# A retention scores step moved, the GroupNorm root in a step of its own, and other first loads and last root, in a two-layer recurrent decoder step

## The chip, the cores and the metric

The kernel runs on one core of one Trainium2 chip, in one launch. The time is device microseconds of an execution, as a median over runs; the profile is one execution recorded on the chip, and its times are microseconds from the start of its span.

## What is computed

One inference step of a hybrid decoder trunk for 256 prompt tokens and 8 x 8 sample tokens, 320 in all, in float32. Each of two layers normalises `x` (2048 wide), projects it with one wide matrix, runs three recurrent branches beside each other, projects each back, weighs the three with sigmoid gates and adds the result to `x`. A last RMSNorm follows. Cut to what the change touches:

```python
def _retention(q, k, v, r0, pos0, gn_g):          # 8 heads, 128 wide, chunks of 128 (or 8) positions
    q = _rope(q, pos); k = _rope(k, pos) * (RET_DK ** -0.5)
    def step(r, inp):
        qc, kc, vc = inp
        sc = jnp.einsum('bihd,bjhd->bhij', qc, kc) * dmask[None]             # scores
        inner = jnp.einsum('bhij,bjhe->bihe', sc, vc)
        cross = jnp.einsum('bihd,bhde->bihe', qc, r) * xi[None, :, :, None]
        r_new = r * g_chunk + jnp.einsum('bjhd,bjhe->bhde', kc * zeta, vc)   # state
        return r_new, inner + cross
    r_last, o = lax.scan(step, r0, (chunks of q, k, v))
    o = ((o - mu) * lax.rsqrt(var + GN_EPS)) * gn_g                          # GroupNorm per head
    return o, r_last

def _layer(x, ...):
    xn = _rmsnorm(x, norm_g)
    proj = xn @ w_in                     # 2048 x 14336: inputs, gate paths and merge gates of all branches
    y_s5, y_lru, y_ret = _s5(...), _rglru(...), _retention(...)
    b_m = (y_m * silu(z_m)) @ w_branch_m          # for the three branches
    merged = sum over m of sigmoid(g_m) * b_m
    return x + merged @ w_out

y = _rmsnorm(x, final_norm_g)            # behind the second layer; the new states are returned too
```

## The kernel before

Tokens lie along the free axis (320), features along the 128 partitions. All large weights stream through the core once. They come in chunks of 512 KB, four k-tiles of 128 by 256 outputs (`raw`, four buffers, issued on SP at L1234). Since the products are to be exact in float32, each half of a chunk is split into a rounded part `whi` (ACT, L126) and a remainder `wlo` (DVE, L99); `prep` and `split` do that into four buffers. Each k-tile and each half of the outputs then takes three matmuls of 128x320: `whi` by the high part of the activations, `whi` by their low part, `wlo` by their high part (L1321, L1322, L1323). A chunk is 24 matmuls.

The order of all engines' work is written by the loop in `stream`, chunk by chunk; the program's scheduler leaves it as it is. `blocks` lists the weight blocks of a layer: inputs of the LRU and S5 branches, gates, then for m = 0 to 3 a pair of retention heads with its q, k, v and z block of four chunks each (16 chunks for each m), the S5 gate path, merges, the GLU, merges, and the output projection. Splits run three halves ahead of the matmuls for most of the program, loads three chunks ahead. After each chunk `self.step()` advances every generator in `self.gens` by one `yield`; so all side work is dealt out in steps of one chunk, and what stands between two yields of a generator is issued in one lump. A block's handler starts one step after its last chunk.

Generators that the change touches or that stand beside it: `ret_qk` rotates q or k: it copies the block out of PSUM (`rraw`), starts the product `ra`, swaps halves of partitions by two DMAs (`rsw`, L840 and L841), multiplies and adds (`ra`, DVE). `ret_heads` loads the decay masks (`rdms`, `rdm`), makes a padded copy `kd` of the keys, then the scores (L894, L895, L898, each set in PSUM of its own), masks them on DVE (`scs`, `rsc`), transposes the keys, loads the old states `r0`, makes the heads' output, its GroupNorm statistics (`bs`, `mv`, L960 and L961), the GroupNorm root (`gv`, a chain of small DVE operations) and the normalised output (`ron`). Behind the statistics it spawns `ret_state`, which makes the new states: L1004, the store `ret_p` (L1018), then four times a pair of masked values `rvm` (DVE), a pair of matmuls L1029 into PSUM and the update `r` (DVE, L119), and after each head the store `ret_s` (L1033, on SP, so it stands in line with the loads of `raw`). The loads of `r0` for the next m wait until `ret_state` of this one has ended. Small PSUM tiles come from a pool of four, main accumulators from a pool of two.

At the start, `constants` and `more_constants` load the vectors `pv` and small tables on ACT's queue, `x` and the first chunk come in alternation on SP, and `x_group(0)` splits the first activations before `prep(0)` splits the first weights. At the end `finish` takes the sum of squares (L1100 adds the last ones), makes the reciprocal root (`ts` on DVE, Ln and Exp on ACT, three DVE operations), multiplies the eight output tiles `yt` (fourteen DVE operations, two on POOL, L1117) and stores each (`y`, L1120).

## Time and profile before

| | before |
|---|---|
| median of 3 runs | 2405.69 us (2404.81 to 2407.02) |
| profiled execution | 2406.62 us, span 2404.8 us |
| mean granted TensorE clock | 0.995 |
| busy | PE 2360.1, DVE 1572.1, ACT 1070.8, POOL 605.9 us |
| HBM | 373.83 MB read, 31.74 MB written, 169 GB/s over the span |

In the profile PE is the matmul engine, DVE the vector engine, ACT the scalar engine, POOL GpSimd, and SP the engine on whose queue most DMAs are issued (SPq). An entry `wlo<-raw,whi` names what an operation writes and reads. PEclk is the share of full clock that TensorE was granted: 1.00 is 2.4 GHz, 0.50 is 1.2 GHz. "Idle before" is the time an engine stood before an operation, with the operation that released it. The tables of waits count such times by line.

### The profile page before, as it was taken

The numbers are of one execution on the slowest core, as the hardware profiler recorded it, in microseconds if no ns is written. First come the engines' busy times: TensorE is split into PE (matmuls) and PEld (weight loads), VectorE is DVE, ScalarE is ACT, GpSimd is POOL, SyncE is SP. The second block draws the span as 40 slices with busy tenths as digits, with TensorE's granted clock in tenths as the row PEclk, the third lists the DMA queues.
The fourth block names the chain that finished last, engine by engine and source line by source line (L and its number), as shares of the span: only waits on it lengthen the run. The fifth ranks groups of instructions, "written<-read, shape, count | busy, mean of one in ns | idle before, by whom it ended". The sixth has DMA issues, their size and how long they took to land.

```text
span 2404.8 us, 44311 instructions
## 1 busy us (share of the span) xinstructions
PE 2360.1 (98%) x16746; PEld 2326.9 (97%) x16746; DVE 1572.1 (65%) x2900; ACT 1070.8 (45%) x1941; POOL 605.9 (25%) x1157
## 2 busy tenths in 40 slices
PE   8999999999999999999999999999999999999997
PEld 8999999889999999999999999999999999999997
DVE  7889466876774756755567665767776656555544
ACT  6655344333343434444555554433333334444443
POOL 2004001999920000300100000699950200000011
PEclk9999999999999999999999999999999999999998
DMA  6655587454654545446656587454555554444553
GB/s 213 220 173 166 159 218 211 126 172 159 193 171 164 168 151 173 152 151 195 201 165 190 162 223 206 147 182 137 168 170 168 178 184 157 149 153 146 158 179 118
DMA packets 153590, 413.71 MB, mean 172 GB/s; under 512 B 18592, under 2 KB 59296, under 8 KB 153120
## 3 DMA queue, kind: packets, MB, share of 16 engines
q1 hardware_dynamic: 152656, 410.58, 54.1%
q8 instruction: 131, 2.15, 0.4%
q14 instruction: 83, 0.68, 0.1%
q10 hardware_dynamic: 720, 0.30, 0.0%
HBM read 373.83 MB, written 31.74 MB: 169 GB/s over the span
## 4 chain that ended last, share of the span: by engine, by line
PE 95%; DVE 3%; DMA 1%; issue 0%; ACT 0%; SPq 0%; ACTq 0%; DVEq 0%
PE pt L1321 30%; PE pt L1323 29%; PE pt L1322 29%; DMA raw<-w_in 1%; PE ps L638 1%; PE ps L757 1%; DVE wlo L99 1%; DVE rvm L99 1%; PE ps L546 1%; PE ps L1029 1%; PE ps L894 0%; PE ps L953 0%; ACT whi L126 0%; DVE yt L99 0%; PE ps L1004 0%
## 5 line engine op out<-in xcount | busy, mean ns | idle before, releaser
L99 DVE TENSOR_TENSOR wlo<-raw,whi 128x512 fp32r<-128x512 f32 x1187 | 845.5, 727 | 758.1 <-ACT whi L126 737.4
L126 ACT ACTIVATE whi<-raw 128x512 fp32r<-128x512 f32 x1187 | 737.7, 629 | 1071.3 <-PE pt L1322 894.2
L1321 PE MATMUL pt<-xh,whi 128*128 128x320 f32 x3320 | 1037.5, 313 | 6.1 <-ACT whi L126 6.1
L1323 PE MATMUL pt<-xh,wlo 128*128 128x320 f32 x3320 | 1029.8, 310 | 7.6 <-DVE wlo L99 7.5
L1322 PE MATMUL pt<-xl,whi 128*128 128x320 f32 x3320 | 1027.6, 310 | 0.0
L1321 PEld LDWEIGHTS pt<-xh,whi 128*128 128x128 f32 x3320 | 625.6, 188 | 11.8 <-ACT whi L126 6.4
L1323 PEld LDWEIGHTS pt<-xh,wlo 128*128 128x128 f32 x3320 | 625.0, 188 | 11.5 <-DVE wlo L99 11.3
L1322 PEld LDWEIGHTS pt<-xl,whi 128*128 128x128 f32 x3320 | 625.4, 188 | 2.8
L1321 PE MATMUL pt<-yhl,whi 128*128 128x320 f32 x756 | 234.7, 310 | 0.0
L1323 PE MATMUL pt<-yhl,wlo 128*128 128x320 f32 x756 | 233.6, 309 | 0.0
L1322 PE MATMUL pt<-yhl,whi 128*128 128x320 f32 x756 | 233.6, 309 | 0.0
L563 POOL TENSOR_TENSOR cs<-H,l2r 128x64 f32<-128x64 f32 x254 | 121.2, 477 | 255.6 <-DVE H L113 235.9
L252 POOL TENSOR_TENSOR acc<-acc,sq 128x320 f32<-128x320 f32 x28 | 25.6, 914 | 586.4 <-ACT sq L126 585.4
L1321 PE MATMUL pt<-M,whi 128*128 128x320 f32 x512 | 158.7, 310 | 0.0
L1323 PE MATMUL pt<-M,wlo 128*128 128x320 f32 x512 | 158.2, 309 | 0.0
L1322 PE MATMUL pt<-M,whi 128*128 128x320 f32 x512 | 158.2, 309 | 0.0
L1321 PEld LDWEIGHTS pt<-yhl,whi 128*128 128x128 f32 x756 | 141.9, 188 | 0.8 <-issue 0.5
L1322 PEld LDWEIGHTS pt<-yhl,whi 128*128 128x128 f32 x756 | 141.9, 188 | 0.0
L1323 PEld LDWEIGHTS pt<-yhl,wlo 128*128 128x128 f32 x756 | 141.9, 188 | 0.0
L565 POOL TENSOR_TENSOR cs<-cs,H 128x64 f32<-128x64 f32 x254 | 132.3, 521 | 0.0
L564 POOL TENSOR_TENSOR cs<-H,l2i 128x64 f32<-128x64 f32 x254 | 123.8, 487 | 0.0
L566 POOL TENSOR_TENSOR H<-cs,cs 128x64 f32<-128x64 f32 x254 | 117.7, 463 | 19.9
(251 smaller groups left out, 2526.5 us busy)
## 6 DMA issues: line engine op xcount, KB each, us to landing
raw<-w_in SPq DMA_DIRECT2D x447, 512.0 KB, 4.4
raw<-w_out SPq DMA_DIRECT2D x64, 512.0 KB, 4.5
raw<-wb_lru SPq DMA_DIRECT2D x32, 512.0 KB, 4.7
raw<-wb_ret SPq DMA_DIRECT2D x32, 512.0 KB, 3.8
raw<-wb_s SPq DMA_DIRECT2D x32, 512.0 KB, 3.6
r<-sret SPq DMA_DIRECT2D x16, 512.0 KB, 8.0
ret_s<-r SPq DMA_DIRECT2D x16, 512.0 KB, 3.0
raw<-w_glu SPq DMA_DIRECT2D x16, 512.0 KB, 3.6
```

The source lines that it names most:

```text
L99: self.nc.vector.tensor_tensor(o, a, b, op=op)
L126: self.nc.scalar.activation(o, a, f, **k)
L252: self.nc.gpsimd.tensor_tensor(self.acc, self.acc, sq, op=OP.add)
L546: self.nc.tensor.matmul(pp[g][:, a * HN:(a + 1) * HN], wst[:, a, g * 128:(g + 1) * 128], ust[:, 2 * a + g], start=True, stop=True, skip_gr ...
L563: g.tensor_tensor(t1, old, lr, op=OP.mult)
L564: g.tensor_tensor(t2, self.swap(old), li, op=OP.mult)
L565: g.tensor_tensor(t1, t1, new, op=OP.add)
L566: g.tensor_tensor(new, t1, t2, op=OP.add)
L638: nc.tensor.matmul(o[q * 32:(q + 1) * 32], w[:, c, m], H[:, q0 + m, c, col:col + HN], start=col == 1 and c == 0, stop=c == 1, tile_positio ...
L1321: nc.tensor.matmul(o, hi[:, kk, cs], xh, start=k == 0, stop=False)
L1322: nc.tensor.matmul(o, hi[:, kk, cs], xl, start=False, stop=False)
L1323: nc.tensor.matmul(o, lo[:, kk, cs], xh, start=False, stop=k == nk - 1)
```

## The change

In words: (1) `ret_heads` has one more `yield` between the padded copy of the keys and the scores; the third score product goes to the last 128 columns of the first score tile, so that two PSUM tiles are taken and not three. (2) A `yield` between the GroupNorm statistics and the root; `ret_state` is spawned behind the root and its yield. (3) At the start: eight products of `ones` with itself on PE (L216); the first `x` group and `pv` on ACT's queue, in the pieces column 0, `pv`, column 1, columns 2 and 3; the first chunk in four parts on SP; the first weights are split by k-tile between the pieces of `x`, and the first half chunk's matmuls go by k-tile; the tables `ident`, `sm`, `pmask` and the second `pv` are loaded on SP after chunk 8. (4) At the end: `rsqrt_of` takes the root with one activation function on ACT (its table is loaded earlier) and three DVE operations, the last of which leaves the root in PSUM; DVE multiplies from there, ACT copies it to SBUF for POOL, which has four of the sixteen multiplications now.

```diff
@@ -207,23 +207,24 @@
         pc = self.pc
         for l in range(DEPTH):
             self.pv[l] = pc.tile([128, NPV], F32, name=f"pv{l}")
-        nc.scalar.dma_start(self.pv[0], I['pv'][0])
         self.ones = pc.tile([128, 128], F32, name="ones")
         nc.vector.memset(self.ones, 1.0)
         self.fv = self.pl.tile([128, 4, 4], F32, name="fv", tag="fv")
         nc.vector.memset(self.fv, 1.0)
+        p = self.ps()
+        for _ in range(8):
+            nc.tensor.matmul(p[:, :128], self.ones, self.ones, start=True, stop=True)
 
     def more_constants(self):
         nc, I = self.nc, self.I
-        self.table_of(AF.Ln)
         self.ident = self.pc.tile([128, 128], F32, name="ident")
         self.sm = self.pc.tile([128, NK], F32, name="sm")
         self.pmask = self.pc.tile([128, 128], F32, name="pmask")
-        nc.scalar.dma_start(self.ident, I['c_ident'])
-        nc.scalar.dma_start(self.sm, I['c_sm'])
-        nc.scalar.dma_start(self.pmask, I['c_pair'])
+        nc.sync.dma_start(self.ident, I['c_ident'])
+        nc.sync.dma_start(self.sm, I['c_sm'])
+        nc.sync.dma_start(self.pmask, I['c_pair'])
         for l in range(1, DEPTH):
-            nc.scalar.dma_start(self.pv[l], I['pv'][l])
+            nc.sync.dma_start(self.pv[l], I['pv'][l])
 
     def pcol(self, l, key, i):
         c = PV[key] + i
@@ -275,10 +276,16 @@
         self.stt(r, t, 1.5, r, OP.add, OP.mult)
 
     def rsqrt_of(self, p):
+
         r = self.pl.tile([128, T], F32, name="rstd", tag="rstd")
-        for _ in self.rsqrt_steps(p, r):
-            pass
-        return r
+        v, t, q = (self.vt([128, T]) for _ in range(3))
+        rp = self.ps()[:, :T]
+        self.act(q, p[:, :T], AF.Abs_reciprocal_sqrt, scale=1.0 / D, bias=self.fv[:, 2, 0:1])
+        self.ts(v, p[:, :T], 1.0 / D, OP.mult, EPS, OP.add)
+        self.mul(t, q, q)
+        self.stt(t, t, -0.5, v, OP.mult, OP.mult)
+        self.stt(rp, t, 1.5, q, OP.add, OP.mult)
+        return r, rp
 
     def rs2(self, n=2):
         return self.rstd[:, None, :].to_broadcast([128, n, T])
@@ -286,11 +293,17 @@
     def x_load(self, q):
         a = self.py.tile([128, 4, T], F32, name="xin", tag="y")
         self.xin[q] = a
+        if q == 0:
+            for c in range(2):
+                self.nc.scalar.dma_start(a[:, c], self.I['x'][0][:, c])
+                yield
+            self.nc.scalar.dma_start(a[:, 2:4], self.I['x'][1])
+            return
         for h in range(2):
             self.nc.sync.dma_start(a[:, 2 * h:2 * h + 2], self.I['x'][2 * q + h])
             yield
 
-    def x_group(self, q):
+    def x_group(self, q, step=2):
 
         for c in range(4):
             k = 4 * q + c
@@ -300,7 +313,7 @@
             self.copy(xh, x, scale=g)
             self.stt(xl, x, g, xh.bitcast(F32), OP.mult, OP.subtract)
             self.xh[k], self.xl[k] = xh, xl
-            if c % 2:
+            if c % step == step - 1:
                 yield
 
     def x_rest(self, q):
@@ -888,14 +901,15 @@
         q, k = self.ret.pop(('q', m)), self.ret.pop(('k', m))
         kd = self.vt([128, 2, 2, 64], name="rkd")
         self.copy(kd, k[:, :, None, SEQ:].to_broadcast([128, 2, 2, 64]))
+        yield
         pp, sc = [], []
         for n in range(2):
             p = self.ps()
             nc.tensor.matmul(p[:, :256], k[:, n, 0:128], q[:, n, 0:256], start=True, stop=True)
             nc.tensor.matmul(p[:, 256:384], k[:, n, 128:256], q[:, n, 128:256], start=True, stop=True)
             pp.append(p)
-        p = self.ps()
-        nc.tensor.matmul(p[:, :128], kd.rearrange("p n r t -> p (n r t)")[:, 64:192], q[:, :, SEQ:], start=True, stop=True)
+        p = pp[0][:, 384:]
+        nc.tensor.matmul(p, kd.rearrange("p n r t -> p (n r t)")[:, 64:192], q[:, :, SEQ:], start=True, stop=True)
         yield
         scs = self.scs
         for n in range(2):
@@ -960,7 +974,7 @@
                 nc.vector.bn_stats(bs[:, s], o[:, s])
                 nc.vector.bn_aggr(mv[:, n, s], bs[:, s])
         self.flag['av', l, m] = True
-        self.spawn(self.ret_state(l, m, kt, kz, vt, vs, r0))
+        yield
         vv = self.pl.tile([128, 3, 6], F32, name="gv", tag="gv")
         v, rs, t = (vv[:, i] for i in range(3))
         gp = sm[:, K_GP + 6 * m:K_GP + 6 * m + 6]
@@ -970,6 +984,7 @@
         self.rsqrt_vec(rs, v, t)
         self.mul(rs, rs, gp)
         yield
+        self.spawn(self.ret_state(l, m, kt, kz, vt, vs, r0))
         on = []
         for n in range(2):
             x = self.wt([128, 3, 128], name="ron")
@@ -1083,7 +1098,8 @@
                 self.sumsq(y[:, n])
                 self.copy(y[:, n], y[:, n], scale=self.pcol(l, 'fin', 2 * j + n))
             if j == 5:
-                self.table_of(AF.Ln)
+                self.nc.vector.memset(self.fv[:, 2, 0:1], EPS)
+                self.table_of(AF.Abs_reciprocal_sqrt)
             if j == 6:
                 yield 3
                 p = self.fsum = self.ps()
@@ -1107,16 +1123,18 @@
 
     def finish(self):
         nc, O = self.nc, self.O
-        r = self.rsqrt_of(self.fsum)
+        rs, r = self.rsqrt_of(self.fsum)
         for j in (0, 1, 2, 7, 3, 4, 6, 5):
             y = self.ytok[j]
             for n in range(2):
                 if j == 7:
                     self.stt(y[:, n], y[:, n], self.pcol(DEPTH - 1, 'fin', 14 + n), r, OP.mult, OP.mult)
-                elif j > 4 and n:
-                    nc.gpsimd.tensor_tensor(y[:, n], y[:, n], r, op=OP.mult)
+                elif j > 2 and n:
+                    nc.gpsimd.tensor_tensor(y[:, n], y[:, n], rs, op=OP.mult)
                 else:
                     self.mul(y[:, n], y[:, n], r)
+            if j == 0:
+                self.copy(rs, r)
             nc.sync.dma_start(O['y'][j], y)
 
 
@@ -1272,20 +1290,28 @@
                 run(fn, a)
 
         self.constants()
-        for _ in zip(self.x_load(0), load(0, 2)):
-            pass
-        self.more_constants()
+        x0 = self.x_load(0)
+        next(x0)
+        nc.scalar.dma_start(self.pv[0], self.I['pv'][0])
+        list(x0)
+        list(load(0, 4))
+        self.table_of(AF.Ln)
         x = [self.x_load(q) for q in range(1, 4)]
         for i in range(1, 4):
             load_all(i)
             if i == 2:
                 list(x[0])
         self.norm_begin()
-        group = self.x_group(0)
-        next(group)
-        prep(0)
+        group = self.x_group(0, 1)
+        hi = self.phl.tile([128, 2, 256], F32R, name="whi", tag="whi")
+        lo = self.phl.tile([128, 2, 256], F32R, name="wlo", tag="wlo")
+        for k in range(2):
+            next(group)
+            self.split(hi[:, k], lo[:, k], raw[0][:, k])
+        hl[0] = hi, lo
         next(group)
         prep(1)
+        list(group)
         prep(2)
         norm = self.norm_end()
         done = []
@@ -1312,8 +1338,8 @@
                     prep(nprep)
                     nprep += 1
                 hi, lo = hl.pop(2 * i + h)
-                for n in range(2):
-                    for kk in range(2):
+                for n, kk in ((0, 0), (1, 0), (0, 1), (1, 1)) if i + h == 0 else ((0, 0), (0, 1), (1, 0), (1, 1)):
+                    if 1:
                         k = 4 * c + 2 * h + kk
                         xh, xl = b[2](0, k), b[2](1, k)
                         o = pt[n][:, :T] if nb < 3 else pt[:, n, :T]
@@ -1323,6 +1349,8 @@
                         nc.tensor.matmul(o, lo[:, kk, cs], xh, start=False, stop=k == nk - 1)
             if i in (1, 3, 6, 9):
                 self.x_rest(i // 3)
+            if i == 8:
+                self.more_constants()
 
             if done and i >= done[0][0]:
                 run(*done.pop(0)[1:], now=True)
```

How the order of instructions moves, at three places. On SP in layer 0, for m = 1 (heads 2 and 3): `ret_p` and `ret_s` are state stores, `rsw` the swapped halves of a rotation, `rdms` and `rdm` the decay masks, `r_6707`, `r_6709` the new states of the two heads. Before:

```order
L1018 DMA ret_p<-rp 128x256
L840 DMA rsw<-rraw 64x640
L841 DMA rsw<-rraw 64x640
L1234 DMA raw<-w_in 128x1024 x3
L883 DMA rdms<-c_dms 128x64
L885 DMA rdm<-c_dm 128x2x256
L1234 DMA raw<-w_in 128x1024
L1033 DMA ret_s<-r_6707 128x1024
L840 DMA rsw<-rraw 64x640
L841 DMA rsw<-rraw 64x640
L1234 DMA raw<-w_in 128x1024 x4
L1033 DMA ret_s<-r_6709 128x1024
```

After, at the same place (the states are `r_6755` and `r_6757`):

```order
L853 DMA rsw<-rraw 64x640
L854 DMA rsw<-rraw 64x640
L1252 DMA raw<-w_in 128x1024 x3
L896 DMA rdms<-c_dms 128x64
L898 DMA rdm<-c_dm 128x2x256
L1033 DMA ret_p<-rp 128x256
L1252 DMA raw<-w_in 128x1024
L853 DMA rsw<-rraw 64x640
L854 DMA rsw<-rraw 64x640
L1252 DMA raw<-w_in 128x1024 x3
L1048 DMA ret_s<-r_6755 128x1024
L1252 DMA raw<-w_in 128x1024 x4
```

The first `ret_s` moved from ahead of the second pair of `rsw` (the rotation of k) to three weight loads behind it, and `ret_p` from ahead of the first pair to behind the masks.

On DVE in layer 0, at the scores of m = 1, with the state update of m = 0 beside them (`r_5911`; `rvm` the masked values, `ra` the rotated keys, `rv` the values). Before:

```order
L99 TENSOR_TENSOR wlo<-raw,whi 128x512 x2
L119 SCALAR_TENSOR_TENSOR r_5911<-r_5911,ps 128x512
L99 TENSOR_TENSOR rvm<-rkv,sm 128x512 x2
L99 TENSOR_TENSOR ra<-ra,rsw 128x640
L99 TENSOR_TENSOR wlo<-raw,whi 128x512 x2
L99 TENSOR_TENSOR rv<-pt,rstd 128x640
L99 TENSOR_TENSOR wlo<-raw,whi 128x512 x2
L99 TENSOR_TENSOR scs<-ps,rdms 64x4x16 x2
L99 TENSOR_TENSOR rsc<-ps,rdm 128x256
L99 TENSOR_TENSOR rsc<-ps,rdm 128x128
```

After (the states of m = 0 are `r_5964` and `r_5966`):

```order
L99 TENSOR_TENSOR wlo<-raw,whi 128x512 x4
L99 TENSOR_TENSOR scs<-ps,rdms 64x4x16 x2
L99 TENSOR_TENSOR rsc<-ps,rdm 128x256
L99 TENSOR_TENSOR rsc<-ps,rdm 128x128
L99 TENSOR_TENSOR rsc<-ps,rdm 128x256
L99 TENSOR_TENSOR rsc<-ps,rdm 128x128
L119 SCALAR_TENSOR_TENSOR r_5966<-r_5966,ps 128x512
L99 TENSOR_TENSOR rvm<-rkv,sm 128x512 x2
L99 TENSOR_TENSOR wlo<-raw,whi 128x512 x4
```

A state update and a pair of `rvm`, which stood ahead of `ra` before, now stand behind the score masks.

On DVE at the end of the program, from the final root on (`vt` is scratch, `yt` the output tiles). Before:

```order
L115 TENSOR_SCALAR vt<-ps 128x320
L99 TENSOR_TENSOR vt<-rstd 128x320
L119 SCALAR_TENSOR_TENSOR vt<-vt 128x320
L119 SCALAR_TENSOR_TENSOR rstd<-vt,rstd 128x320
L99 TENSOR_TENSOR yt<-yt,rstd 128x320 x6
L119 SCALAR_TENSOR_TENSOR yt<-yt,pv_112,rstd 128x320 x2
L99 TENSOR_TENSOR yt<-yt,rstd 128x320 x6
```

After:

```order
L115 TENSOR_SCALAR vt<-ps 128x320
L99 TENSOR_TENSOR vt<-vt 128x320
L119 SCALAR_TENSOR_TENSOR vt<-vt 128x320
L119 SCALAR_TENSOR_TENSOR ps<-vt 128x320
L99 TENSOR_TENSOR yt<-yt,ps 128x320 x6
L119 SCALAR_TENSOR_TENSOR yt<-yt,pv_112,ps 128x320 x2
L99 TENSOR_TENSOR yt<-yt,ps 128x320 x4
```

The multiplications take the root from PSUM, and two fewer stand on DVE.

## Rows read from the trace of the kernel before

**Rows 1.** The page, part 1: busy time, share of the span and instructions by engine.

```profile
PE 2360.1 (98%) x16746; PEld 2326.9 (97%) x16746; DVE 1572.1 (65%) x2900; ACT 1070.8 (45%) x1941; POOL 605.9 (25%) x1157
```

**Rows 2.** PE's waits, 411 to 497 us: line, releaser, total us, times, longest.

```profile
PE pt L1323 <- DVE wlo L99: 4.4, 5, 2.9
PE ps L894 <- DVE ra L99: 2.6, 1, 2.6
```

**Rows 3.** PE's waits in the same form, 497 to 1900 us.

```profile
PE ps L894 <- DVE ra L99: 7.9, 5, 2.2
PE pt L1323 <- DVE wlo L99: 3.1, 5, 0.8
PE ps L1029 <- DVE rvm L99: 1.6, 7, 0.5
```

**Rows 4.** Timeline of PE: start, duration, operation, idle before and releaser.

```profile
494.19 0.70 PE L894 MATMUL ps<-ra 128*128 128x256 f32 x2 [2.59 <-DVE ra L99]
...
563.81 0.70 PE L894 MATMUL ps<-ra 128*128 128x256 f32 x2 [2.01 <-DVE ra L99]
```

**Rows 5.** Stretches: length, busy time of each engine, PEclk, DMA share, GB/s.

```profile
453.00:456.00 3.00, 3.00 (x14) 2.96 (x14) 3.00 (x9) 0.44 (x1) 2.69 (x7) 0.53 0.68 145
563.80:570.00 6.20, 6.19 (x30) 5.90 (x31) 2.92 (x4) 1.59 (x4) 5.65 (x15) 0.72 0.00 1
1749.50:1753.00 3.50, 3.43 (x11) 3.07 (x12) 2.99 (x5) 0.94 (x2) 3.27 (x7) 0.51 0.01 5
```

**Rows 6.** Timeline of SP, 540 to 566 us.

```profile
552.31 0.34 SPq L1033 DMA_DIRECT2D ret_s<-r  x1
...
554.01 6.35 SPq L1234 DMA_DIRECT2D raw<-w_in  x4
```

**Rows 7.** Timeline of ACT, 556 to 566 us.

```profile
559.42 1.16 ACT L126 ACTIVATE whi<-raw 128x512 fp32r<-128x512 f32 x2 [4.65 <-DMA raw<-w_in]
```

**Rows 8.** Timeline of DVE, 556 to 566 us.

```profile
558.29 0.95 DVE L99 TENSOR_TENSOR rsw<-rsw,ropr 128x640 f32<-128x640 f32 x1 [3.14 <-DMA rsw<-rraw]
...
560.70 0.68 DVE L119 SCALAR_TENSOR_TENSOR r<-r,ps 128x512 f32<-128x512 f32 x1
561.30 1.58 DVE L99 TENSOR_TENSOR rvm<-rkv,sm 128x512 fp32r<-128x512 f32 x2
```

**Rows 9.** Timeline of DVE, 440 to 458 us.

```profile
442.80 0.29 DVE L960 BATCH_NORM_STATS2 bs<-ps 128x6 f32<-128x128 f32 x1
...
445.49 0.17 DVE L99 TENSOR_TENSOR gv<-mv,sm 128x6 f32<-128x6 f32 x1
...
451.88 1.57 DVE L99 TENSOR_TENSOR wlo<-raw,whi 128x512 fp32r<-128x512 f32 x2
```

**Rows 10.** DVE's forms, 410 to 720 us: count, busy us, mean ns, idle before.

```profile
L99 DVE TENSOR_TENSOR rsc<-ps,rdm 128x256 f32<-128x256 f32 x8 | 3.4, 420 | 0.1
```

**Rows 11.** Chain of work that ended last, 0 to 14 us: start, length, what.

```profile
6.12 0.64 PE pt L1321
...
11.75 0.27 PE pt L1322
...
12.27 0.15 PE pt L1321
```

**Rows 12.** Timeline of ACT, 0 to 14 us.

```profile
9.46 1.15 ACT L126 ACTIVATE whi<-raw 128x512 fp32r<-128x512 f32 x2 [1.52 <-DMA raw<-w_in]
```

**Rows 13.** Chain of work that ended last, 2380 to 2405 us.

```profile
2393.45 2.62 DVE yt L99 x3
...
2398.20 2.41 DVE yt L99 x6
```

**Rows 14.** Timeline of DVE, 2386 to 2405 us.

```profile
2388.94 0.49 DVE L115 TENSOR_SCALAR vt<-ps 128x320 f32<-128x320 f32 x1 [1.08 <-PE ps L1100]
```

**Rows 15.** Timeline of POOL, 2386 to 2405 us.

```profile
2393.59 2.13 POOL L1117 TENSOR_TENSOR yt<-yt,rstd 128x320 f32<-128x320 f32 x2 [14.99 <-DVE rstd L119]
```

**Rows 16.** Stretches, in the columns of rows 5, near the end.

```profile
2402.00:2403.00 1.00, 0.00 (x0) 0.00 (x0) 0.00 (x0) 0.00 (x0) 0.00 (x0) 0.50 1.04 402
```

## The prediction

> **What bounds the kernel now.** I read the page's busy line first: PE is busy 98% of the span [rows 1], so time can only come from the 45 us in which it is not busy, or from matmuls that run on the low clock. Of the 45 us, 6.1 lie before the first matmul and about 16 behind the last, from the final root to the end of the span (the rows of both ends stand with their parts below); that leaves some 22 inside. Next I read PE's waits, split where the first retention stage of layer 0 ends. In that stage PE waits 4.4 us for `wlo` and 2.6 for the rotated `ra` [rows 2]; after it 12.6 us, of which 7.9 are five waits of the scores L894 for `ra` [rows 3]. Third, the clock. Two pauses of 2.9 us (on `wlo`, in the first stage) and 2.0 us (on `ra`) are followed by stretches of 3 and 6.2 us at a granted clock of 0.53 and 0.72, and one near 1749 us by 3.5 us at 0.51 [rows 4, 5]. The lost clock is 3.0 x 0.47 + 6.2 x 0.28 + 3.5 x 0.49 = 1.4 + 1.7 + 1.7 = 4.8 us. A pause of 2.59 us cost nothing of the kind: its first L894 product took 0.70 us, the same as the one at 563.81 that still ran at full clock [rows 4]. So the middle offers 7.0 + 12.6 + 4.8 = **24.4 us**, the two ends some 22, and the 2360 us of matmuls nothing.
>
> Why the scores wait is read from four engines around 552 us. SP stands at `ret_s` L1033 until 552.31 and only then issues the two `rsw` copies of the k rotation and the next weights [rows 6]. ACT, out of weights, then stands 4.65 us for a `raw` [rows 7]. DVE gets its `rsw` at 558.29, does two `wlo`, the state update `r` (0.68) and two `rvm` (1.58) that came due meanwhile, and reaches `ra` last [rows 8]; PE has meanwhile run dry and stands 2.01 us at the scores [rows 4].
>
> **The scores one step later, the root in a step of its own, ret_state later.** A step is a weight chunk, 24 matmuls of 0.147 us = 3.5 us. These three edits remove no operation worth naming: the third score product goes to the free 128 columns of the first PSUM tile. They only re-deal steps. (1) The scores have one more step, 3.5 us, behind `ra`, against a longest wait of 2.2 to 2.6; and the k rotation's `rsw` no longer stands behind a `ret_s` on SP (order above: `rsw`, three `raw`, then `ret_s`). The five later waits of 7.9 us should go, and with them the clock loss of 1.7 + 1.7 behind two of them: −11.3. (2) The GroupNorm batch begins at 442.80, its root runs from 445.49 to 448.9, and the next `wlo` starts only at 451.88, 9 us after the batch began: two and a half steps' worth of DVE time in one step [rows 9]. With a yield between, 2.7 us of statistics and 3.4 us of root each meet a step of their own with two `wlo` (1.57 each pair). The later `wlo` waits of 3.1 us should go to nearly nothing: −3.1. (3) `ret_state` is now three steps later against the rest (one for the scores, two for the root's yields). What is late next is told by DVE's order above: the second pair of `rvm` now comes in the same step as the score masks (two `rsc` of 0.42 [rows 10], four smaller operations; an estimate of 1.8 together) and the update `r` 0.68, together with its own 1.58 [rows 8]: 4.1 us of DVE against a step of 3.5, with two `wlo` pairs more, and right behind a `raw` that SP holds back at `ret_s`. PE's matmul L1044 (L1029 before) stands in order behind them, with the next main matmuls queued behind it. The trace has no such step. From below: the present L1029 waits are 0.1 to 0.5 us [rows 3]. From above: the score waits, up to 2.2 us with a lost clock of 1.7. I take about 1 us at each of the six changes from one m to the next, 6.3 us in all, in place of the present 1.6: **+4.7**. Sum after the first stage: −11.3 − 3.1 + 4.7 = −9.7.
>
> In the first stage the S5 chain (`cb`, `H`) fills DVE too. There the split takes away the lump at the GroupNorm but not the load; of its 7.0 + 1.4 I give half of the longest pause, 2.9 us: −1.5. **Middle: −11**, with ends −4 (the new waits are as long as the old, with one lost clock) and −20 (no new waits).
>
> **The head.** PE's first matmul is at 6.12; until 12.2 the chunk's matmuls come every 0.27 us, from then on every 0.15 [rows 11]. Eight dummy products on `ones` need no load and so fill part of 1.1 to 6 us (the nearest row is L894, the same kind of product with twice the columns, 0.70 us with its drain at full clock [rows 4]; half the columns at half the clock I estimate at 0.45 each, 3.5 us for the eight). If they count towards the rise, it comes some 5 us earlier, at about 7 in place of 12, and the first chunk's 21 slow matmuls win up to 20 x 0.12 = 2.4 us. But the second chunk can't start before its `raw`: ACT waited for it until 9.46 [rows 12]; with one `wlo` behind that is about 10 against 12.7 now. So −2.6 at best; if the pause between the last dummy and the first `xh` (about 1.3 us) takes the clock back, only the loads' order is left, −0.3. The other moves here are the loads: `x` and `pv` go to ACT's queue in an order by need, and four constants to SP at step 8, 4 issues of 0.4 us that lie behind three `raw` chunks already under way: nothing. I take **−1.8**. The Trainium skill, "TensorE: Matmul & The Clock Gate", section "What's actually happening", says that the throttled state is the default and that activity releases it, at a point that varies from run to run; by that the dummies do count, and the gain would lie at the −2.6 end. Here a pause of 2.59 us kept the clock and one of 2.01 lost it [rows 4, 5], so a pause of 1.3 us is not safe, which the page's variation agrees with.
>
> **The tail.** Now the root is `ts`, Ln, a table load, Exp and three DVE operations from 2388.94 to 2393.45 [rows 13, 14]. After: the root on ACT beside `ts` (in DVE's order behind it, 0.5), three operations of 0.5: ready 2388.9 + 0.5 + 0.5 + 1.5 + gaps of 0.03 to 0.1 = 2391.6, **−1.8**. The multiplications: the first three took 2.62 us beside POOL's pair (2.13 for two [rows 15]), the last six 2.41 [rows 13], 0.87 and 0.40 each. POOL has four now and DVE twelve instead of fourteen, with one operand from PSUM (0.42 each, an estimate from the 0.40). The copy of `r` to SBUF stands between: DVE's third waits for it, about 0.6. DVE: 2 x 0.42 + 0.6 + 4 x 0.42 + 2 x 0.5 + 4 x 0.42 = 5.8, done at 2397.4 against 2400.6; POOL: 4 x 1.07 from 2393.0, done at 2397.3. But the stores, 2.6 MB, move at the full 402 GB/s in the last stretch [rows 16]: 6.5 us after the first, whoever is done. First store some 2.5 us earlier (2392.5 against 2395.04), so end −2.3; ends −1.0 (POOL slows DVE as now) and −3.8. The Trainium skill, "SBUF — State Buffer", section "Who interferes with whom", has a DVE operation with two SBUF inputs contend with a GpSimd operation that reads SBUF, and with at most one not. By that the new form runs at 0.42 beside POOL; without it, at 0.87, DVE would end 2 us later and the tail would gain 1.0.
>
> **Sum.** −1.8 − 11.2 − 2.3 = −15.3. The profiled run took 2406.62 for its span of 2404.8, so 2391.3 for the changed one; it lies 0.9 above the median of the runs shown, 2405.69, and the difference applied to that median gives **2390.4 us**, −0.64%.
>
> **The rivals.** *The wait moves and is not shortened:* the six L1044 waits and the `raw` behind `ret_s` take 2 us each and the clock falls behind two or three of them; then the middle gains 2, the ends 4: 2399.6. For it: SP is held at `ret_s` as often as before, and the order still has `raw` right behind. Against: the k rotation no longer depends on it. *All inner waits vanish*, the first stage's too, with the clock loss, but for 2.4 us that the first stage keeps: 2405.7 − 22 − 4 = 2379.7. For it: a step of 3.5 us exceeds every wait that is there. Against: the S5 chain's load stays. *Slower:* in the eight retention stages the later `ret_state` meets the next m's masks and GroupNorm. Its place is DVE's first `rvm` pair at L1044; it decides when DVE is over one step (3.5 us) late there, for then PE stands as long as on `wlo` in the first stage, 2.9 us, and loses 1.4 to 1.7 of clock: 8 x 4.5 = 36 less the 20 of old waits and 4 of ends, +12: 2418. For it: the 4.1 us step above. Against: DVE is then only 0.6 us over, and the step after has slack. *The dummies do nothing* costs 1.5 and lies inside the forecast.
>
> **How the numbers follow.** Forecast (2384 to 2396) 0.60; wait moved (2396 to 2402) 0.20; all waits gone (2378 to 2384) 0.14; slower 0.06. The range, 2381 to 2400, leaves out the slower case, the lower half of the third case and the end of the second, about 0.2. About 0.2% (4.8 us) is what a measurement can tell from no change: faster, below 2400.9, takes the forecast, the third and two thirds of the second, 0.87; same, the rest of the second, 0.07; slower 0.06.
>
> **What the profile of the changed kernel would show.** Right: no wait of L908 (the scores) on `ra`; waits of L1044 on `rvm` near 1 us six times; later `wlo` waits under 0.5 in all; clock 1.00 throughout behind 500 us; matmul pitch 0.15 from 7 us on; first `y` store 3.6 us behind the start of `ts` (now 6.1), DVE multiplications of 0.42 beside POOL. Wrong: a score wait that is still there, a clock below 0.8 behind L1044, or SP's wait at `ret_s` L1048 that holds a `raw` for which ACT then stands over 3.5 us.

## The result and the profile after

| | before | after |
|---|---|---|
| median | 2405.47 us (4 runs, 2404.81 to 2407.02) | 2385.31 us (4 runs, 2384.99 to 2385.83) |
| ratio of after to before | | 0.9915, 95% interval 0.9898 to 0.9933 |
| profiled execution | 2406.62 us, span 2404.8 | 2385.83 us, span 2383.5 |
| mean granted clock | 0.995 | 0.997 |

The change gains 20.2 us; 15.3 were forecast, and 2385.31 lies in the stated range of 2381 to 2400. Both programs run the same 14,976 main matmuls in the same order, so the two traces can be matched matmul by matmul. Behind its first chunk the changed kernel is 1.7 us ahead, from the fifth chunk to the first retention stage 0.9, and at the last main matmul 18.65 us. Behind that its span ends 13.3 us after the last sum of squares, against 16.0. So the head gives 0.9 us, the two retention parts together 17.8 (9.3 in layer 0, 8.5 in layer 1), the tail 2.65.

PE's waits in the profile after, from 411 to 497 us, to be read against [rows 2]; the columns are total us, times, and the longest:

```profile
PE ps L1044 <- DVE rvm L99: 3.4, 1, 3.4
PE pt L1349 <- DVE wlo L99: 1.9, 2, 1.6
```

The kernel before has a third line there, beside the two of [rows 2]:

```profile
PE ps L1029 <- DVE rvm L99: 1.4, 6, 0.3
```

The same table from 497 to 1900 us, against [rows 3]:

```profile
PE ps L967 <- DMA r<-sret: 3.1, 7, 0.7
PE ps L1044 <- DVE rvm L99: 1.2, 5, 0.3
```

The scores (L908 now) wait nowhere. Behind 497 us the waits on `wlo` are gone, and those on `rvm` have not grown. Two lines are new: one long wait of L1044 in the first stage, and 3.1 us in which the heads' products L967 wait for the old states `r`, a DMA. At the new long wait stands the only fall of the clock in the middle. The stretch around it, with PEclk the third figure from the end:

```profile
472.00:482.00 10.00, 7.50 (x31) 6.95 (x32) 7.65 (x13) 1.26 (x2) 9.30 (x19) 0.66 0.60 181
```

And the start of it in PE's timeline:

```profile
474.50 1.54 PE L1044 MATMUL ps<-rvm,rkv 128*128 128x512 f32 x2 [3.45 <-DVE rvm L99]
475.84 0.47 PE L1347 MATMUL pt<-xh,whi 128*128 128x320 f32 x1
476.11 0.47 PE L1348 MATMUL pt<-xl,whi 128*128 128x320 f32 x1
```

The matmuls behind it stand 0.27 us apart, as in the first microseconds of the program [rows 11]; 10 x 0.34 = 3.4 us are lost. DVE's timeline of the changed kernel shows the lump that PE waits for: the rotation's product, the low part of the output, the four operations of the S5 update and the masked values in one row, with no idle time between (idle time would stand in brackets):

```profile
469.95 0.81 DVE L99 TENSOR_TENSOR ra<-pt,ropr 128x640 f32<-128x640 f32 x1
470.69 0.81 DVE L99 TENSOR_TENSOR yhl<-z,yhl 128x640 fp32r<-128x640 f32 x1
471.42 0.67 DVE L99 TENSOR_TENSOR cb<-H,l2r 128x256 f32<-128x256 f32 x1
...
473.13 0.63 DVE L99 TENSOR_TENSOR H<-H,cb 128x256 f32<-128x256 f32 x1
473.66 1.53 DVE L99 TENSOR_TENSOR rvm<-rkv,sm 128x512 fp32r<-128x512 f32 x2
```

The end in DVE's timeline of the changed kernel, against [rows 13, 14]:

```profile
2370.90 0.49 DVE L115 TENSOR_SCALAR vt<-ps 128x320 f32<-128x320 f32 x1 [1.71 <-ACT vt L126]
...
2372.35 0.50 DVE L119 SCALAR_TENSOR_TENSOR ps<-vt 128x320 f32<-128x320 f32 x1
2372.89 0.89 DVE L99 TENSOR_TENSOR yt<-yt,ps 128x320 f32<-128x320 f32 x2
2374.28 1.68 DVE L99 TENSOR_TENSOR yt<-yt,ps 128x320 f32<-128x320 f32 x4 [0.50 <-ACT rstd L126]
```

And in POOL's, against [rows 15]:

```profile
2374.32 3.33 POOL L1133 TENSOR_TENSOR yt<-yt,rstd 128x320 f32<-128x320 f32 x4 [14.37 <-ACT rstd L126]
```

The root stands in PSUM at 2372.85; the four multiplications that DVE makes while POOL works beside it take 0.42 us each.

### The profile page after: what moved, and what is told of

Same layout as the page of the kernel before. It is cut to its first block, busy times and chain, and to the rows that moved or that the text cites. A ratio compares the mean times of both kernels' runs of the same rounds, so it can differ in the third digit from the quotient of the medians.

```text
span 2383.5 us, 44361 instructions
## 1 busy us (share of the span) xinstructions
PE 2356.6 (99%) x16762; PEld 2327.0 (98%) x16762; DVE 1569.4 (66%) x2900; ACT 1070.6 (45%) x1941; POOL 618.5 (26%) x1159
## 4 chain that ended last, share of the span: by engine, by line
PE 77%; DMA 2%; DVE 1%; issue 0%; ACT 0%; DVEq 0%; ACTq 0%
PE pt L1347 25%; PE pt L1349 24%; PE pt L1348 24%; DMA r<-sret 2%; PE ps L651 1%; PE ps L1044 1%; PE ps L770 0%; DVE rvm L99 0%; PE ps L559 0%; PE ps L1019 0%; PE ps L908 0%; PE ps L967 0%; PE ps L1003 0%; PE ps L643 0%; DVE yt L99 0%; PE ps L909 0%
## 5 line engine op out<-in xcount | busy, mean ns | idle before, releaser
L99 DVE TENSOR_TENSOR wlo<-raw,whi 128x512 fp32r<-128x512 f32 (+1 forms) x1188 | 845.2, 727 | 746.9 <-ACT whi L126 729.9
L126 ACT ACTIVATE whi<-raw 128x512 fp32r<-128x512 f32 (+1 forms) x1188 | 738.1, 629 | 1074.6 <-PE pt L1348 939.8
L577 POOL TENSOR_TENSOR cs<-H,l2i 128x64 f32<-128x64 f32 x254 | 132.7, 522 | 0.0
```

The lines of the kernel that those rows point to most:

```text
L99: self.nc.vector.tensor_tensor(o, a, b, op=op)
L126: self.nc.scalar.activation(o, a, f, **k)
L577: g.tensor_tensor(t2, self.swap(old), li, op=OP.mult)
```

## Where the 17.8 us of the middle went

The listed waits between 411 and 1900 us fall from 21.0 us (29 of them) to 9.6 (15): 11.4 us. The clock's loss there, summed over the stretches at half clock, falls from 5.1 us (three of 3.4 us) to 3.4 (one of 6.8): 1.7 us. That leaves 4.7 us, and the timeline of PE around one wait shows most of it. This is the wait on `wlo` in the first stage of the changed kernel:

```profile
454.65 0.31 PE L1347 MATMUL pt<-xh,whi 128*128 128x320 f32 x1
454.80 0.31 PE L1348 MATMUL pt<-xl,whi 128*128 128x320 f32 x1
456.71 0.41 PE L1349 MATMUL pt<-xh,wlo 128*128 128x320 f32 x1 [1.60 <-DVE wlo L99]
456.96 0.31 PE L1347 MATMUL pt<-xh,whi 128*128 128x320 f32 x1
457.11 0.30 PE L1348 MATMUL pt<-xl,whi 128*128 128x320 f32 x1
```

Matmuls start every 0.147 us but are drawn 0.31 us long, so the idle time in brackets begins only when the drawn end is over. Without the stop the third would have started at 454.95 and the fourth at 455.09; it started at 456.96. The stop cost 1.87 us where 1.60 are listed: 0.27 more. Fourteen stops fewer are some 3.8 us by that one row (an estimate). The Trainium skill, "Perfetto Trace Analysis", section "Tensor Engine Instruction (MATMUL, LD_WEIGHTS)", says that the end of a TensorE instruction is computed and not observed; that agrees with drawn lengths twice the pitch here. About 1 us of the middle stays without an entry.

## The experiments

Nine kernels ran several times beside the kernel before; three ran once beside one run of it and have no interval. The kernel before took 2406.3 to 2407.8 us in the medians beside them, and its single runs lie between 2402.7 and 2409.6, so the ratio is what counts.

**Part 1 alone: the scores one step later.**

```diff
 kernel before, ret_heads
         self.copy(kd, k[:, :, None, SEQ:].to_broadcast([128, 2, 2, 64]))
+        yield
...
-        p = self.ps()
-        nc.tensor.matmul(p[:, :128], kd...[:, 64:192], q[:, :, SEQ:], start=True, stop=True)
+        p = pp[0][:, 384:]
+        nc.tensor.matmul(p, kd...[:, 64:192], q[:, :, SEQ:], start=True, stop=True)
```

> The kernel before with the first part of the change alone: the scores one step later, the third score product in the first PSUM tile. Theory A (the scores waited because they followed the rotation too closely, and a state store held up the rotation's copies on SP): the five later waits of the scores, 7.9 us, and the clock lost behind two of them, 3.4, go, the GroupNorm waits of 3.1 us stay: 11 us gained, about 2394. Rival B (the gain needs the GroupNorm split too, since DVE's lump only moves on): under 5 us gained, over 2400, with new waits of PE on DVE in place of the old ones.

Measured: 2395.37 us, ratio 0.9959 (0.9945 to 0.9974), a gain of some 10 to 11 us. The size is theory A's, the make-up neither's. The scores waits are gone, but those on `wlo` too, and PE waits more on the masked values (L1030 here), 5.0 us against 1.6 before, as rival B has it. All of PE's waits from 497 to 1900 us:

```profile
PE ps L1030 <- DVE rvm L99: 5.0, 9, 1.0
PE ps L989 <- DVE ron L115: 0.3, 1, 0.3
```

This part does more than give the scores room. `ret_heads` spawns `ret_state`, so one step more in it delays the state generator too, and on SP the first `ret_s` now stands behind the rotation's copies and a weight load:

```profile
544.89 0.47 SPq L840 DMA_DIRECT2D rsw<-rraw  x1
545.41 0.59 SPq L841 DMA_DIRECT2D rsw<-rraw  x1
546.09 0.54 SPq L1235 DMA_DIRECT2D raw<-w_in  x1
552.12 0.35 SPq L1034 DMA_DIRECT2D ret_s<-r  x1
```

No run here gives the scores their step and leaves the store where it was.

**Part 2 alone: the root in a step of its own and `ret_state` behind it.**

```diff
 kernel before, ret_heads
         self.flag['av', l, m] = True
-        self.spawn(self.ret_state(l, m, kt, kz, vt, vs, r0))
+        yield
...
         self.mul(rs, rs, gp)
         yield
+        self.spawn(self.ret_state(l, m, kt, kz, vt, vs, r0))
```

> The kernel before with the second part alone: the yield between GroupNorm statistics and root, and the state generator spawned behind the root's step. Theory A (the parts are separate): the waits on the low weights behind the GroupNorm go, 3.1 us after 497 us and 3 to 4 with the clock in the first stage, and the waits of the scores stay: 6 to 7 us gained, about 2399. Rival B (the later state store leaves SP's queue ahead of the rotation of the keys free, so the scores waits go with this part as well): 15 us or more gained, 2391 or less, with the scores waits under 2 us in all.

Measured: 2387.16 us, ratio 0.9923 (0.9909 to 0.9938): 19 us, nearly the whole gain. Rival B holds and theory A falls: the scores, which this kernel leaves where they were, no longer wait behind the first stage. All of PE's waits from 497 to 1900 us:

```profile
PE ps L1030 <- DVE rvm L99: 1.1, 5, 0.3
```

No clock is lost in this kernel between 400 and 1900 us. SP's timeline shows what moved for the scores. At this place the kernel before stood at `ret_s` until 552.31 with the rotation's copies and the next weights behind it [rows 6]; SP's waits of the kernel before, 530 to 560 us, have for it:

```profile
SPq L1033 <- DVE r L119: 8.7, 1, 8.7
```

In this kernel:

```profile
542.51 0.47 SPq L840 DMA_DIRECT2D rsw<-rraw  x1
543.03 0.59 SPq L841 DMA_DIRECT2D rsw<-rraw  x1
543.71 1.21 SPq L1235 DMA_DIRECT2D raw<-w_in  x2
553.42 0.34 SPq L1034 DMA_DIRECT2D ret_s<-r  x1
```

SP still stands at the store, for 8.4 us, but the copies have left before it, and PE does not wait for the weights behind it.

**The split without the move.** Part 2 is two edits; here `ret_state` is spawned where it was and only the yield is added.

```diff
 kernel before, ret_heads
         self.spawn(self.ret_state(l, m, kt, kz, vt, vs, r0))
+        yield
```

> The kernel before with the yield between GroupNorm statistics and root alone; the state generator is spawned where it was, so SP's order is that of before. Theory A (what the second part gains in the later stages comes from the state store that left its place ahead of the key rotation's copies): only the waits on the low weights behind the GroupNorm go, 4 to 7 us gained, 2399 to 2402, and the scores still wait for the rotated keys, 8 us or more. Rival B (it comes from the GroupNorm's lump on DVE): 15 us or more gained, scores waits under 3 us.

Measured: 2404.81 us, ratio 0.9991 (0.9982 to 1.0001), not told apart from no change. Theory A holds in its main point, with less gained than it said: the waits of the scores stay, and those on `wlo` fall to 1.2 us. The two largest lines of PE's waits from 497 to 1900 us:

```profile
PE ps L894 <- DVE ra L99: 9.5, 5, 2.5
PE pt L1324 <- DVE wlo L99: 1.2, 3, 0.5
```

In the first stage the lump comes back one step later: behind a wait of 3.0 us 8 us at a clock of 0.57, and again 4 us behind a scores wait of 2.8, at the place where one of 2.59 kept the clock [rows 4]. The two stretches:

```profile
460.00:468.00 8.00, 6.98 (x29) 6.75 (x30) 7.93 (x16) 0.78 (x2) 7.45 (x15) 0.57 0.50 143
494.00:498.00 4.00, 4.00 (x17) 3.59 (x16) 2.54 (x4) 0.54 (x2) 3.69 (x9) 0.57 0.00 0
```

**Only SP's order.** The stores of the states are issued three steps later, and nothing else is moved: `ra` still stands behind the state update and `rvm` on DVE.

```diff
 kernel before, ret_state
-            nc.sync.dma_start(O['ret_s'][l, h], r0[n])
+            self.spawn(self.ret_store(O['ret_s'][l, h], r0[n]))
+    def ret_store(self, o, r):
+        yield 2
+        self.nc.sync.dma_start(o, r)
```

> The kernel before with nothing moved but the state stores on SP: each is issued three steps later, so the first one of a pair of heads stands behind the key rotation's copies and three weight loads, as in the changed kernel; DVE's and PE's order stay. Theory A: the scores waits of 7.9 us after the first stage and the clock lost behind them go, 11 us gained, about 2395. Rival B (the rotated keys are late because DVE makes the state update and the masked values ahead of them): the scores waits stay over 5 us, under 3 us gained.

Measured: 2394.18 us, ratio 0.9949 (0.9934 to 0.9964), 12 to 13 us. Theory A holds. The scores wait nowhere behind 497 us, in a kernel in which they stand where they stood, and no clock is lost there. PE's waits from 497 to 1900 us:

```profile
PE pt L1327 <- DVE wlo L99: 4.5, 6, 0.8
PE ps L1029 <- DVE rvm L99: 2.2, 9, 0.6
```

So the long waits of the scores were SP's: the store held up the rotation's copies and the weights behind them. The Trainium skill, "DMA: Bandwidth & Descriptors", section "Anatomy of one DMA — SWDGE (gpsimd) path", says that DMA engines do not wait on semaphores and that a wait is the issuing sequencer's, before dispatch. The section is on another path than SP's; on SP the 8.7 us above stand on the issuing queue too, and taking the stores out of the way gave 12 to 13 us.

**The change without part 1, beside the change.** All of the change but the scores' step and tile; and the changed kernel again on the same chip.

> The changed kernel without its first part (the scores stand where they stood before), all else as changed. Theory A (the second part alone frees the scores, and the first part only pushes the state generator into the first stage's load): faster than the changed kernel by 1 to 4 us, about 2382, with no wait over 2 us behind 411 us and no clock lost. Rival B (the first part adds its own gain): slower than the changed kernel by 3 us or more.

> The changed kernel itself, beside the others on the same chip: 2385 to 2386, the ratio that the result shows.

Measured: 2386.25 us, ratio 0.9915 (0.9898 to 0.9931), against 2385.01, ratio 0.9910 (0.9895 to 0.9925). Neither theory: part 1 is worth about 1 us beside part 2, and the intervals lie on each other. Without it no clock is lost between 400 and 1900 us and the first stage's longest wait is 1.5 us; with it the scores don't wait in the first stage either (1.4 us here), but L1044 waits 3.4 there.

**The head alone, and the tail alone.** Each is the kernel before with the functions of that end as changed.

> The kernel before with the new first loads, the dummy products and the tables on SP alone. Theory A (read from the two traces, where the matmuls of the fourth chunk on run 0.9 us ahead of before): 0.9 us gained, 2404.6. Rival B (the step of the prediction): 1.8 us gained, 2403.7.

> The kernel before with the new last root and its multiplications from PSUM alone. Theory A: the stretch from the last sum of squares to the end shortens as between the two traces, 15.96 to 13.3: 2.6 us gained, 2402.8. Rival B (the table load in the step of the sixth output block delays weights): under 1.5 us gained.

The 0.9 us of the first text hold from the fifth chunk on. Head: 2405.84 us, ratio 0.9997 (0.9988 to 1.0007): no gain that can be seen. Tail: 2403.73 us, ratio 0.9991 (0.9981 to 1.0000); in its trace the last main matmul ends where it did before, and the span is 2.6 us shorter, as theory A has it.

What became of the dummies is told by all the profiles of this study together. In the six without them the first main matmul starts at 5.99 to 6.39 us and the slow pitch of 0.27 us lasts until 9.5 to 12.25. In the eight with them the start is at 5.55 to 6.33, and there are two cases. In four, the changed kernel's own profile and the head alone among them, the first main matmuls still run slowly and the slow pitch ends at 9.2 to 10.6. In the other four the granted clock rises on record at 3.9 to 4.9 us, ahead of the first main matmul, which is drawn 0.41 us long and not 0.63; in one of these (the change without part 1), where PE stood 1.8 us between the last dummy and the first main matmul, it falls back at 7.5 (0.50 over 8 to 10 us), and the pitch is slow until 10.9. (PEclk reads 1.00 ahead of the first change on record, so the pitch tells the clock there.) The first main matmul of the changed kernel:

```profile
5.57 0.63 PE L1347 MATMUL pt<-xh,whi 128*128 128x320 f32 x1 [0.73 <-ACT whi L126]
```

And that of a kernel of the second case, the one named below with two steps more:

```profile
5.55 0.41 PE L1349 MATMUL pt<-xh,whi 128*128 128x320 f32 x1 [1.11 <-ACT whi L126]
```

But the seventh chunk starts at 29.1 to 30.1 us (mean 29.5) without, and at 29.1 to 30.5 (mean 29.6) with them. In this last kernel the chain of work that ended last runs over a weight load. Its row:

```profile
6.12 8.32 DMA raw<-w_in
```

In the changed kernel PE, 1.7 us ahead by then, stops in the fourth chunk for the low part of the second `x` group, which ACT began to round at 16.2 us as in the kernel before:

```profile
19.11 0.42 PE L1348 MATMUL pt<-xl,whi 128*128 128x320 f32 x1 [0.36 <-DVE xl L119]
```

So what sets the pace next are the loads and the splits behind them.

**The first stage's wait.** The changed kernel with one yield, or two, ahead of the masked values of layer 0, m = 0.

```diff
 changed kernel, ret_state
         nc.sync.dma_start(O['ret_p'][l][:, 2 * m:2 * m + 2], rp)
+        if l == 0 and m == 0:
+            yield 1            # in the second kernel: yield 2
         for n in range(2):
```

> The changed kernel with one more yield ahead of the masked values, in the first stage of layer 0 alone (l = 0, m = 0). Theory A (the 3.4 us wait of L1044 and the clock lost behind it come from the masked values standing in one step with the S5 update and the low parts of the output): that wait falls under 2 us and no clock is lost: 4 to 6 us gained on the changed kernel, about 2380. Rival B (DVE is late in this stage as a whole, whatever the order): a wait of about 3 us on the low weights takes its place, no gain.

> The same with two more steps. Theory A: as with one, within 1 us. Rival B: slower than with one, since the masked values now meet the rotation of the next keys or the next stage's r0 loads come later.

Measured in one run each: 2382.91 and 2380.89 us, beside 2407.49 for the kernel before. No clock is lost in either between 400 and 1900 us. The 3.4 us wait is replaced by one of 1.6 on `wlo`, so theory A holds for the clock, and for the time with two steps (4.4 us under the changed kernel's first median) rather than with one (2.4). The second text has neither case: two steps were 2 us faster than one, not within 1 us and not slower. With one step, 2.4 us of waits on `rvm` come at later changes of m; with two, 0.8. PE's waits of the kernel with two steps, 411 to 497 us:

```profile
PE pt L1351 <- DVE wlo L99: 3.5, 3, 1.6
PE ps L1046 <- DVE rvm L99: 0.2, 1, 0.2
```

**The heads behind the loads of the old states.**

```diff
 changed kernel, ret_heads
             r0.append(r)
-        yield
+        yield 2 if m else 1
         while not self.flag.get(('v', l, m)):
```

> The changed kernel with the heads' products one step later for m above 0, behind the loads of the old states. Theory A (the 3.1 us in which PE waits for these loads is the price of the later state generator): these waits go, 2 to 3 us gained, about 2382.5. Rival B (the chain from states to loads to heads is longer than the 16 steps of one m, so the delay returns at the next m): the waits return in part, or new waits of L1044 come, under 1 us gained.

Measured in one run: 2383.9 us, 1.4 under the changed kernel's first median, between the theories. The waits on `r` are gone; 3.7 us of waits on `rvm` and `wlo` stand behind 497 us in place of 1.2. The last run puts both remedies together.

> The changed kernel with both: the masked values of the first stage two steps later, and the heads' products one step later for m above 0. Theory A (the two waits are separate, and what the later heads cost is small): 1 to 2 us below the better of the two, 2379 to 2380, ratio to before 0.989. Rival B (what the heads' delay gives it takes back at the next changes of m, as new waits on the masked values): 2381 or more, no better than the first of the two alone.

Measured: 2389.30 us (2386.92 to 2391.58), ratio 0.9924 (0.9911 to 0.9938): above the single run of either, and by the medians worse than the changed kernel (the intervals of the ratios overlap). Rival B holds: the waits come back on DVE, and one of 1.5 us costs clock again. PE's waits from 497 to 1900 us:

```profile
PE pt L1351 <- DVE wlo L99: 4.2, 5, 1.3
PE ps L1046 <- DVE rvm L99: 3.3, 7, 1.5
PE pt L1349 <- ACT whi L126: 1.0, 1, 1.0
```

The kernel with two steps more in the first stage alone is the fastest that ran, 2380.89 us, in its single run.

## Why the prediction was right, and where it was not

*The scores.* That the five waits and the clock loss behind them go was right: −11.3 in the sum, and the changed kernel has none. Of the two reasons given, SP's store ahead of the rotation's copies is the one that is shown to count: moved alone it gave 12 to 13 us. The step's room, named first, is hardly needed: without it the change is about 1 us slower. Part 1 alone and part 2 alone each move the store as well, since both start `ret_state` later, so their gains of 10 to 11 and 19 us do not add up. Part 2, to which the sum gave 3.1 and 1.5 us, gives nearly the whole gain without the other.

*The GroupNorm split.* The later `wlo` waits went from 3.1 us to none, as put. The reason given is not shown, though: with the yield alone 1.2 us of them stay and the time can't be told apart from before, and with part 1 alone, which has no split, they go too. That the number came out is in part luck.

*The new waits at L1044, +4.7.* This is the step that failed. About 1 us at each of six changes of m was put; measured are five waits of at most 0.3, 1.2 in all, less than before, so the term was 5.1 us off. The DVE work in the step with the score masks was counted nearly right (4.1 us; the masks, `r` and `rvm` run from 499.16 to 502.71, 3.6), but DVE was not behind when it began. At the first change, whose rows follow, it had just stood 3.9 us for its weights (3.0 at the next), and PE lost 0.24 us:

```profile
498.32 0.91 DVE L99 TENSOR_TENSOR wlo<-raw,whi 128x512 fp32r<-128x512 f32 x1 [3.88 <-ACT whi L126]
...
501.28 1.43 DVE L99 TENSOR_TENSOR rvm<-rkv,sm 128x512 fp32r<-128x512 f32 x2
```

A lump only costs what exceeds the slack that DVE has at its start.

*The first stage, −1.5, and the slower rival.* The waits fell from 8.4 us to 5.3 and the clock's loss rose from 1.7 to 3.4: −1.4, which meets the −1.5 by luck, as the sum had no new wait there. The slower rival's mechanism is there: DVE is more than a step late at `rvm`, PE stands 3.45 us and 3.4 us of clock go, where 2.9 and 1.4 to 1.7 were put. It happens in one of eight stages, the one in which the S5 update shares DVE; that load is what the prediction held against "all inner waits vanish". Layer 0 still gains 9.3 us in all.

*The price of the stops.* The sum took the listed waits at face value. Some 0.27 us a stop, fourteen times, is the second part of what it lacked, 3.8 us by that estimate.

*The old states' loads, not in the sum.* SP's loads of `r0` follow the end of `ret_state`, which is later now; 3.1 us of waits on them are new. They were put nowhere, and took back a part of the gain.

*The head, −1.8.* The matched traces have 1.7 behind the first chunk and 0.9 from the fifth on; the head alone gives nothing that can be seen. Whether the dummies count differs from profile to profile. The sum limited the gain by the second chunk's load and looked no further; the wait for the second `x` group takes back half of it.

*The tail, −2.3.* Measured 2.65 in the matched traces. The root is ready 2.66 us after the last sum of squares against 4.58: −1.9, where −1.8 was put. The multiplications from PSUM took 0.42 each beside POOL, as put. The first store is issued 3.6 us behind the last sum of squares, where the sum had it; behind the start of `ts`, from which the forecast counted, it is 2.9, since `ts` waits for ACT now. That a DVE operation with one SBUF operand is not held up by POOL (the rule of the Trainium skill that the prediction cites, "SBUF — State Buffer", section "Who interferes with whom") is what these rows show: 1.68 us for four while POOL worked, against 2.62 for three [rows 13].

*The signs.* Two of the three signs of being wrong are in the profile of the changed kernel: the clock below 0.8 behind L1044, and ACT standing over 3.5 us for a `raw` that SP issued behind a `ret_s` (at 490.86):

```profile
497.66 1.15 ACT L126 ACTIVATE whi<-raw 128x512 fp32r<-128x512 f32 x2 [4.59 <-DMA raw<-w_in]
```

The second cost PE nothing that shows: its next stop is the one of 0.24 us at 502.76. Of the signs of being right, the pitch of 0.15 from 7 us on did not come (9.2), and the L1044 waits near 1 us did not either.

*The sum.* −15.3 forecast, −20.2 measured: head 0.9 too much, middle 6.6 too little, tail 0.35 too little, against 21.3 us between the two profiled spans (the medians lie 20.2 apart). The middle's 6.6 are 5.1 at L1044 and 4.7 that no listed wait has, less 3.1 for the old states and 0.1 in the first stage.

## What to carry to other kernels

A queue that issues in order makes every waiting entry a gate: look for stores that wait for late results ahead of small copies on the way to the matmul engine, and try to move the store before you move the consumer. A step's load on an engine says little by itself; it costs what it exceeds the slack at that point, so one extra step can free seven stages and hurt the eighth, and two remedies that look good singly (one run each here) can undo each other. Clearing one resource at the start of a program (the clock) shows nothing while the loads and splits behind it set the pace.

## What was not expected of the hardware

A stop of the matmul engine cost 0.27 us more than the wait listed for it in the row shown, since matmuls are drawn 0.31 us long at a pitch of 0.147. The clock fell behind a wait of 1.5 us (the last kernel, 0.72 over 556 to 562 us, with one of 1.3 three us ahead of it) and stayed up behind another of 1.5 (part 2 alone, with one of 1.1 three us ahead) and one of 2.59 [rows 4]. Where it falls is not fixed either: of the two kernels whose middle is that of before, the head alone lost it at 563, 635 and 1751 us and the tail alone at 1679 and 1751, and neither behind its wait of 3.1 us in the first stage. With 3.4 to 3.8 us of dummy products in front, it was up before the first main matmul in four profiles of eight. The stretch of the last kernel, in the columns of [rows 5]:

```profile
556.00:562.00 6.00, 5.75 (x26) 5.38 (x27) 5.13 (x8) 0.94 (x3) 5.53 (x11) 0.72 0.47 126
```
